# Splitting a weight chunk in two operations per helper engine rather than four

## The chip, the cores and the metric
The kernel runs on one core of one Trainium2 chip, as one launch. The metric is the device time of that launch in microseconds. A core has engines that work side by side, each in its own order and tied to the others by semaphores: TensorE (PE) for matmuls, with its weight loads shown apart as PEld; VectorE (DVE), ScalarE (ACT) and GpSimd (POOL) for elementwise work; SyncE (SP), which here issues nearly all loads.

## The reference
Two blocks run one after the other on 256 rows of 1024 features, all in float32. The first has two layers: modulated RMS norms, a mixer (differential attention beside neighbourhood attention in the first layer, grouped-query attention with sinks in the second), and a SwiGLU feed-forward; a context of 256 rows goes along in the first layer. The second block has four layers, and each of them is, cut to what matters:

```
for i in range(4):
    y = mixer_i(x)              # windowed attention, recurrent (RG-LRU), latent attention (MLA), windowed
    x = layer_norm(ALPHA * x + y, ...)
    x = layer_norm(ALPHA * x + cross_attention(x, mem_k, mem_v, x_w_q[i], x_w_o[i]), ...)
    h = causal_depthwise_conv(x @ f_w_up[i], ...)       # width 3, 2 x 2816 columns
    g, u = split(h)
    x = layer_norm(ALPHA * x + (silu(g) * u) @ f_w_down[i], ...)
```

Nearly all of the arithmetic is a product of 256 rows with a weight matrix that is used once. So every weight is read from HBM once, some 400 MB in all.

## The kernel before
**Products in two parts.** A float32 operand is written as hi + lo, where hi is its value in the engine's reduced float32 format (`F32R`) and lo what is left over. `mm3` (L137) then makes a product of three matmuls: hi by hi, hi by lo, lo by hi (L139, L140, L141). Activations are split by `split` (ACT makes hi at L157, DVE makes lo at L158), weights by `weights` (L125). A few first products of a stage skip the split and use plain float32 matmuls (`fp32_groups`, L110).

**Weights in chunks.** A weight matrix comes in chunks of 128 partitions by up to 2048 columns (1 MB). `raw` allocates a raw tile from a pool and SP loads it; `weights` allocates a hi and a lo tile and fills them piece by piece. For each piece ACT copies raw to hi (L133, tile `whi`), and DVE then subtracts hi from raw (L134, tile `wlo`). The piece width is set by one line:

```
h = (n // 4 + 63) // 64 * 64
```

With n = 2048 that gives four pieces of 512 columns on each engine; the 7 narrower chunks of the MLA block give four of 384 or 320. There are 296 chunks. A matmul waits only for the piece that holds its columns.

**Order.** The program is written stage by stage; a tile scheduler then lays out each engine's instructions in one fixed order. An engine takes them strictly in that order, so an instruction that waits holds up all behind it. `held` and `updates` (L85, L90) are lists of closures by which the program puts the tail of a norm behind later matmuls.

**The places that matter below.** The start of the program splits four chunks of memory weights, with nothing else for PE to do. `layer_norm` (L871) works on two halves of the rows: statistics on DVE (L890, L891), two small POOL operations (`rstd`, L175 and L176), the scaling of the row on DVE (L904, tile `r`), then transposes on PE (L165). `ffn` (L928) makes hidden tiles: `up` gives PSUM banks, `conv` scales them on ACT (L246, tile `cg`) and adds taps on DVE (L250); then SiLU (L954) and a product (L955) give `hf`, which is split into `hh` and `hl`; `down` takes these to the accumulators. The first two hidden tiles come from plain float32 matmuls (banks `s`); the chunks of the third and fourth (f = 2, 3) are split. `rglru` (L1071) has gates on ACT (L1108, L1114, L1115), products on POOL (L1117, L1118) and DVE operations (L1119 to L1121) for four groups, and the chunks of its last four projections are split in between.

Of the kernel before, what the change touches and what calls it, by code (L numbers as in the profile page):

```python
# [58 lines left out]
class Net:  # L59
# [65 lines left out]
    def weights(self, src, n=CW):  # L125
        nc = self.nc
        r = self.raw(src, n)
        hi = self.whl.tile([P, CW], F32R, tag="whi", name="whi")
        lo = self.whl.tile([P, CW], F32R, tag="wlo", name="wlo")
        h = (n // 4 + 63) // 64 * 64  # L130
        for a in range(0, n, h):
            b = min(a + h, n)
            nc.scalar.activation(hi[:, a:b], r[:, a:b], AF.Copy)  # L133
            nc.vector.tensor_tensor(lo[:, a:b], r[:, a:b], hi[:, a:b].bitcast(F32), op=ALU.subtract)  # L134
        return hi, lo
# [1513 lines left out]
```

## Time and profile before
| | |
|---|---|
| median of 3 runs | 2535.28 us (2532.03 to 2540.05) |
| the profiled execution | 2532.42 us; its span 2530.6 us |
| PE busy | 2468.5 us, 98% of the span |
| PEld busy | 2094.9 us, 83% |
| DVE busy | 1701.2 us, 67%, 3602 instructions |
| ACT busy | 1215.5 us, 48%, 2630 instructions |
| POOL busy | 130.8 us, 5% |
| lo pieces (L134) | 1184 instructions, 782.7 us, 688 ns each |
| hi pieces (L133) | 1184 instructions, 663.0 us, 620 ns each |
| mean load from HBM | 166 GB/s |

The page follows one execution. Busy shares are averages over stages; what ended an engine's idle time is named behind an arrow (`<-DVE wlo L134`: idle until that DVE instruction was done). A line of a helper such as L134 stands for all its callers.

### The profile page before, as it was taken

What the parts mean: (1) busy time and instruction counts of PE and PEld (TensorE: products, weight loads), DVE (VectorE), ACT (ScalarE), POOL (GpSimd) and SP (SyncE); (2) the same over time, 40 slices, a digit from 0 to 9 for tenths busy, and PEclk for the clock granted to TensorE, in tenths of its full rate; (3) what the DMA queues carried; (4) which work ended last, traced back from release to release, by engine and by line L of the source; (5) the groups of instructions that cost most, each with busy time, mean ns of one, the idle gap of its engine ahead of it and who ended that gap; (6) DMA issues with size and microseconds to landing.
All of it is one profiled execution on the core that took longest, in us unless ns stands there. A gap on an engine that the chain in (4) does not pass through costs nothing.

```text
span 2530.6 us, 39877 instructions
## 1 busy us (share of the span) xinstructions
PE 2468.5 (98%) x15706; PEld 2094.9 (83%) x15706; DVE 1701.2 (67%) x3602; ACT 1215.5 (48%) x2630; POOL 130.8 (5%) x172
## 2 busy tenths in 40 slices
PE   7999999999999999999999999999999999999998
PEld 5967658777788679986899988999878999769998
DVE  5463674343348765568787789677877777986777
ACT  4242353222235544446455665465555455564664
POOL 2000001111100000000000010000000000000000
PEclk9999999999999999999999999999999999999999
DMA  9415325343223545543545545355344455433653
GB/s 391 170 50 212 123 74 183 138 151 142 95 84 134 212 158 212 195 169 133 183 167 186 189 150 224 117 219 194 135 154 184 151 199 186 171 143 125 234 176 115
DMA packets 63708, 419.31 MB, mean 166 GB/s; under 512 B 7440, under 2 KB 7696, under 8 KB 16928
## 3 DMA queue, kind: packets, MB, share of 16 engines
q1 hardware_dynamic: 62240, 412.56, 44.9%
q0 software_dynamic: 1280, 4.20, 0.5%
q8 instruction: 123, 2.02, 0.3%
q14 instruction: 65, 0.53, 0.1%
HBM read 411.45 MB, written 5.28 MB: 165 GB/s over the span
## 4 chain that ended last, share of the span: by engine, by line
PE 87%; DVE 8%; ACT 3%; issue 1%; POOL 1%; DMA 0%; POOLq 0%; DVEq 0%; ACTq 0%
PE banka L139 9%; PE banka L140 9%; PE banka L141 9%; PE banks L139 6%; PE banks L141 6%; PE banks L140 6%; PE bankb L141 5%; PE bankb L140 5%; PE bankb L139 5%; PE bankt L165 3%; PE banko L139 2%; PE banko L141 2%; PE banks L110 2%; PE banko L140 2%; DVE wlo L134 2%; PE bankt L141 2%
## 5 line engine op out<-in xcount | busy, mean ns | idle before, releaser
L134 DVE TENSOR_TENSOR wlo<-raw,whi 128x512 fp32r<-128x512 f32 (+1 forms) x1184 | 782.7, 688 | 288.0 <-ACT whi L133 285.0
L133 ACT ACTIVATE whi<-raw 128x512 fp32r<-128x512 f32 (+1 forms) x1184 | 663.0, 620 | 638.7 <-issue 175.7
L141 PE MATMUL banks<-Th,wlo 128*128 128x256 f32 x880 | 249.5, 284 | 3.0 <-DVE wlo L134 3.0
L139 PE MATMUL banks<-Th,whi 128*128 128x256 f32 x880 | 249.3, 283 | 0.6 <-DVE uf L250 0.6
L140 PE MATMUL banks<-Tl,whi 128*128 128x256 f32 x880 | 249.1, 283 | 0.0
L141 PEld LDWEIGHTS banks<-Th,wlo 128*128 128x128 f32 x880 | 168.8, 192 | 4.1 <-DVE wlo L134 4.1
L139 PEld LDWEIGHTS banks<-Th,whi 128*128 128x128 f32 x880 | 168.8, 192 | 1.7 <-issue 0.7
L140 PEld LDWEIGHTS banks<-Tl,whi 128*128 128x128 f32 x880 | 168.8, 192 | 0.8
L139 PE MATMUL banka<-whi,Th 128*128 128x512 f32 (+1 forms) x304 | 122.2, 404 | 2.6 <-ACT Th L157 2.0
L140 PE MATMUL banka<-wlo,Th 128*128 128x512 f32 (+1 forms) x304 | 120.1, 398 | 2.0 <-DVE wlo L134 2.0
L655 DVE TENSOR_TENSOR sg<-sg,bankb 128x512 f32<-128x512 f32 x22 | 15.1, 688 | 158.4 <-PE bankb L141 158.4
L141 PE MATMUL banko<-Th,wlo 128*128 128x256 f32 x424 | 120.9, 285 | 0.6 <-DVE wlo L134 0.6
L139 PE MATMUL bankt<-Th,whi 128*128 128x256 f32 x424 | 120.3, 284 | 0.0
L141 PE MATMUL bankt<-Th,wlo 128*128 128x256 f32 x424 | 120.0, 283 | 0.0
L140 PE MATMUL bankt<-Tl,whi 128*128 128x256 f32 x424 | 120.0, 283 | 0.0
L139 PE MATMUL banko<-Th,whi 128*128 128x256 f32 x424 | 120.0, 283 | 0.0
L140 PE MATMUL banko<-Tl,whi 128*128 128x256 f32 x424 | 119.9, 283 | 0.0
L141 PE MATMUL banka<-whi,Tl 128*128 128x512 f32 (+1 forms) x304 | 117.9, 395 | 0.3 <-DVE Tl L158 0.3
L139 PE MATMUL bankb<-Th,whi 128*128 128x256 f32 (+1 forms) x344 | 115.0, 335 | 0.0
L141 PE MATMUL bankb<-Th,wlo 128*128 128x256 f32 (+1 forms) x344 | 114.7, 334 | 0.0
L140 PE MATMUL bankb<-Tl,whi 128*128 128x256 f32 (+1 forms) x344 | 114.2, 332 | 0.0
L157 ACT ACTIVATE hh<-hf 128x256 fp32r<-128x256 f32 x110 | 45.7, 415 | 136.2 <-DVE hf L955 135.2
(489 smaller groups left out, 6355.4 us busy)
## 6 DMA issues: line engine op xcount, KB each, us to landing
raw<-in_f_w_up_dram SPq DMA_DIRECT2D x88, 1024.0 KB, 4.8
raw<-in_ffn_w_dram SPq DMA_DIRECT2D x66, 1024.0 KB, 4.8
adaw<-in_ada_w_dram SPq DMA_DIRECT2D x48, 1024.0 KB, 4.8
raw<-in_f_w_down_dram SPq DMA_DIRECT2D x44, 1024.0 KB, 4.8
raw<-in_x_w_q_dram SPq DMA_DIRECT2D x16, 1024.0 KB, 4.8
raw<-in_x_w_o_dram SPq DMA_DIRECT2D x16, 1024.0 KB, 5.5
raw<-in_w_in_ab_dram SPq DMA_DIRECT2D x12, 1024.0 KB, 5.3
raw<-in_a_w_qkv_dram SPq DMA_DIRECT2D x12, 1024.0 KB, 4.9
```

The source lines that it names most:

```text
L110: self.nc.tensor.matmul(ps[:, f * S + t * P : f * S + (t + 1) * P], r[:, k * n * P + f * P : k * n * P + (f + 1) * P], xv[:, k, ts], start ...
L133: nc.scalar.activation(hi[:, a:b], r[:, a:b], AF.Copy)
L134: nc.vector.tensor_tensor(lo[:, a:b], r[:, a:b], hi[:, a:b].bitcast(F32), op=ALU.subtract)
L139: mm(out, l[0], r[0], start=start, stop=False)
L140: mm(out, l[0], r[1], start=False, stop=False)
L141: mm(out, l[1], r[0], start=False, stop=stop)
L157: nc.scalar.activation(hi, src, AF.Copy)
L165: self.nc.tensor.transpose(out, src, self.ident[:k, :k])
L655: nc.vector.tensor_tensor(sg, sg, ps[1], op=ALU.mult)
```

## The change
Four becomes two: a chunk's hi is made by two ACT operations of 1024 columns and its lo by two DVE operations of 1024 (for the narrower chunks two of 768 or 640). Nothing else is edited.

```
-        h = (n // 4 + 63) // 64 * 64
+        h = (n // 2 + 63) // 64 * 64
         for a in range(0, n, h):
             b = min(a + h, n)
             nc.scalar.activation(hi[:, a:b], r[:, a:b], AF.Copy)
             nc.vector.tensor_tensor(lo[:, a:b], r[:, a:b], hi[:, a:b].bitcast(F32), op=ALU.subtract)
```

DVE and ACT have 592 instructions fewer each; POOL's order is the same, PE's has the same matmuls, with several hundred of them in another place. The scheduler lays the engines' order out anew.

The first place is DVE in the second half of the norm after the first windowed attention (`st`, `mv` and `r` are the norm's tiles). Before:

```order
1073 L889 SCALAR_TENSOR_TENSOR r<-xs,bankb 128x512 x2
1074 L890 BN_STATS st<-r 128x6 x2
1075 L134 TENSOR_TENSOR wlo<-raw,whi 128x512
1076 L891 BN_AGGR mv<-st 128x2
1077 L134 TENSOR_TENSOR wlo<-raw,whi 128x512
1078 L904 TENSOR_SCALAR r<-r,mv,rs 128x512 x2
```

The changed kernel's DVE in the same place:

```order
1034 L889 SCALAR_TENSOR_TENSOR r<-xs,bankb 128x512 x2
1035 L890 BN_STATS st<-r 128x6 x2
1036 L134 TENSOR_TENSOR wlo<-raw,whi 128x1024
1037 L891 BN_AGGR mv<-st 128x2
1038 L158 TENSOR_TENSOR Tl<-xv,Th 128x4x128
1039 L904 TENSOR_SCALAR r<-r,mv,rs 128x512 x2
```

A piece of 1024 columns now stands ahead of L891, and the lo of an activation (Tl, 512 columns) in place of a weight piece behind it.

The second place is ACT at the start of the feed-forward of the second layer of the second block; the same pattern stands at the other three. Before:

```order
740 L157 ACTIVATE Th<-xv 128x4x128 x2
741 L246 ACTIVATE cg<-banks,fm 128x256 x2
742 L133 ACTIVATE whi<-raw 128x512
743 L954 ACT_TABLE_LOAD
744 L954 ACTIVATE hf<-cg 128x256
745 L246 ACTIVATE cg<-banks,fm 128x256 x2
746 L157 ACTIVATE hh<-hf 128x256
747 L133 ACTIVATE whi<-raw 128x512 x3
748 L954 ACTIVATE hf<-cg 128x256
749 L133 ACTIVATE whi<-raw 128x512 x4
```

The changed kernel's ACT there:

```order
716 L157 ACTIVATE Th<-xv 128x4x128 x2
717 L133 ACTIVATE whi<-raw 128x1024 x2
718 L246 ACTIVATE cg<-banks,fm 128x256 x2
719 L954 ACT_TABLE_LOAD
720 L954 ACTIVATE hf<-cg 128x256
721 L246 ACTIVATE cg<-banks,fm 128x256 x2
722 L157 ACTIVATE hh<-hf 128x256
723 L133 ACTIVATE whi<-raw 128x1024 x2
724 L954 ACTIVATE hf<-cg 128x256
725 L133 ACTIVATE whi<-raw 128x1024
```

The whole chunk of f = 3 (one piece of it before) now stands ahead of the scaling of the first hidden tile, L246.

The third place is DVE in the recurrent block, at its second and third group. Before:

```order
1437 L1119 TENSOR_SCALAR sq<-r 128x512
1438 L1120 SCALAR_TENSOR_TENSOR a_13812<-a_13812,r 128x512
1439 L134 TENSOR_TENSOR wlo<-raw,whi 128x512
1440 L1121 SCALAR_TENSOR_TENSOR a_13812<-a_13812,r 128x512
1441 L134 TENSOR_TENSOR wlo<-raw,whi 128x512 x2
1442 L1119 TENSOR_SCALAR sq<-r 128x512
1443 L1120 SCALAR_TENSOR_TENSOR a_13915<-a_13915,r 128x512
```

The changed kernel's DVE there:

```order
1351 L1119 TENSOR_SCALAR sq<-r 128x512
1352 L1120 SCALAR_TENSOR_TENSOR a_13166<-a_13166,r 128x512
1353 L134 TENSOR_TENSOR wlo<-raw,whi 128x1024
1354 L1121 SCALAR_TENSOR_TENSOR a_13166<-a_13166,r 128x512
1355 L1119 TENSOR_SCALAR sq<-r 128x512
1356 L1120 SCALAR_TENSOR_TENSOR a_13307<-a_13307,r 128x512
```

Pieces two, three and four of that chunk, which stood around L1121, have become one operation ahead of it, the chunk's second half; the first half stands before this place.

## Rows read from the trace of the kernel before
**Rows 1.** The page's busy times (engine, us, share, instructions) and its chain by engine
```profile
PE 2468.5 (98%) x15706; PEld 2094.9 (83%) x15706; DVE 1701.2 (67%) x3602; ACT 1215.5 (48%) x2630; POOL 130.8 (5%) x172
PE 87%; DVE 8%; ACT 3%; issue 1%; POOL 1%; DMA 0%; POOLq 0%; DVEq 0%; ACTq 0%
```
**Rows 2.** A stretch: its length, busy PE, PEld, DVE, ACT, POOL, then clock, DMA
```profile
2087.70:2151.00 63.30, 63.30 (x466) 60.43 (x465) 44.68 (x88) 36.61 (x75) 0.00 (x0) 1.00 0.53 186
```
**Rows 3.** What PE waited for: us in total, times, longest us
```profile
PE banka L139 <- ACT whi L133: 12.9, 3, 8.8
PE bankt L165 <- DVE r L904: 8.1, 7, 2.2
PE banka L140 <- DVE wlo L134: 4.3, 6, 1.2
PE banks L141 <- DVE wlo L134: 3.4, 6, 1.1
```
**Rows 4.** Groups by shape: busy us, mean ns, idle before and its releasers
```profile
L134 DVE TENSOR_TENSOR wlo<-raw,whi 128x512 fp32r<-128x512 f32 x1156 | 769.1, 692 | 288.0 <-ACT whi L133 285.0
L133 ACT ACTIVATE whi<-raw 128x512 fp32r<-128x512 f32 x1156 | 650.9, 623 | 629.1 <-issue 175.7 <-PE bankb L140 118.0 <-PE banka L140 72.8
```
**Rows 5.** Timeline of the start, DVE and ACT: start us, duration us, operation
```profile
7.52 2.29 DVE L158 TENSOR_TENSOR meml<-raw,memh 128x2048 fp32r<-128x2048 f32 x1 [6.37 <-ACT memh L157]
9.73 2.49 DVE L134 TENSOR_TENSOR wlo<-raw,whi 128x512 fp32r<-128x512 f32 x4
...
5.58 1.91 ACT L157 ACTIVATE memh<-raw 128x2048 fp32r<-128x2048 f32 x1 [3.57 <-DMA raw<-in_memT_dram]
```
**Rows 6.** Timeline of the start, PE's first lo matmuls of two memory chunks
```profile
10.46 0.58 PE L141 MATMUL banka<-memh,wlo 128*128 128x256 f32 x1
...
40.56 0.39 PE L141 MATMUL banka<-memh,wlo 128*128 128x256 f32 x1 [0.22 <-DVE wlo L134]
```
**Rows 7.** Timeline of the first norm of the second block: POOL, DVE, PE
```profile
1206.38 0.19 POOL L175 TENSOR_SCALAR rs<-mv 128x1 f32<-128x1 f32 x1 [75.03 <-DVE mv L891]
...
1216.92 0.52 POOL L175 TENSOR_SCALAR rs<-mv 128x1 f32<-128x1 f32 x1 [9.72 <-DVE mv L891]
...
1216.75 0.63 DVE L134 TENSOR_TENSOR wlo<-raw,whi 128x512 fp32r<-128x512 f32 x1
...
1218.71 0.66 PE L165 MATMUL bankt<-cst,r 128*128 128x128 f32 x4 [1.13 <-DVE r L904]
```
**Rows 8.** Timeline of the second convolution block's start: ACT, DVE, PE
```profile
1641.33 1.02 ACT L246 ACTIVATE cg<-banks,fm 128x256 f32<-128x256 f32 x2 [1.82 <-PE banks L110]
1646.57 0.63 ACT L133 ACTIVATE whi<-raw 128x512 fp32r<-128x512 f32 x1 [4.23 <-DMA raw<-in_f_w_up_dram]
...
1654.52 0.41 DVE L158 TENSOR_TENSOR hl<-hf,hh 128x256 fp32r<-128x256 f32 x1
...
1652.13 0.38 PE L141 MATMUL banko<-Th,wlo 128*128 128x256 f32 x1 [0.55 <-DVE wlo L134]
...
1657.51 0.40 PE L139 MATMUL banka<-whi,hh 128*128 128x512 f32 x1
```
**Rows 9.** Timeline of the recurrent block: DVE, PE
```profile
1512.06 0.68 DVE L134 TENSOR_TENSOR wlo<-raw,whi 128x512 fp32r<-128x512 f32 x1
...
1512.79 0.39 PE L141 MATMUL banks<-Th,wlo 128*128 128x256 f32 x1 [1.13 <-DVE wlo L134]
...
1515.69 0.39 PE L141 MATMUL banks<-Th,wlo 128*128 128x256 f32 x1 [0.71 <-DVE wlo L134]
```
**Rows 10.** Timeline of PE around eight transposes, in a full stretch
```profile
1464.99 0.40 PE L141 MATMUL bankb<-whi,hl 128*128 128x512 f32 x1
1465.22 0.60 PE L165 MATMUL bankt<-cst,r 128*128 128x128 f32 x4
1465.66 0.60 PE L165 MATMUL banko<-cst,r 128*128 128x128 f32 x4
1466.02 0.48 PE L139 MATMUL bankb<-whi,hh 128*128 128x512 f32 x1
```

More of the change, by code (lines that the diff above doesn't have):

```diff
@@ L129, in weights @@
         lo = self.whl.tile([P, CW], F32R, tag="wlo", name="wlo")
-        h = (n // 4 + 63) // 64 * 64
+        h = (n // 2 + 63) // 64 * 64
         for a in range(0, n, h):
```

## The prediction
> **What bounds the kernel now.** I read the page's busy shares and its chain first. TensorE (PE) is busy for 2468.5 of 2530.6 us and carries 87% of the chain that ended last; VectorE (DVE) carries 8%, ScalarE (ACT) 3% [rows 1]. Next came busy time by stretch: in the middle of a feed-forward block PE is busy for 63.30 of 63.30 us while DVE has 44.68 and ACT 36.61 of work [rows 2]. So over most of the span the splitting of weights is hidden, and a saving there buys nothing. Then I read what PE waits for. Its lines that name split pieces are hi for 12.9 us in 3 waits (8.8 of it the start of the program, before anything has been split), lo for 4.3 in 6 and 3.4 in 6; a norm's scaling (`r`, L904) holds it for 8.1 us in 7 waits [rows 3]. Those places decide the sign; the 1184 + 1184 pieces in between do not.
>
> **What a wider piece costs.** A 512-column lo takes 692 ns and hi 623 ns [rows 4]; a 2048-column operation of the same kind takes 2.29 us on DVE and 1.91 on ACT [rows 5]. So 512 more columns cost (2.29 - 0.69)/3 = 0.53 us on DVE and (1.91 - 0.62)/3 = 0.43 on ACT, and a 1024-column piece takes about 1.22 and 1.05 us. Four queued lo pieces take 2.49 us together [rows 5], a step of 0.60 us each; two of 1024 columns take 0.60 + 0.53 + 1.22 = 2.35. That is 0.14 us a chunk, some 40 us of DVE over 296 chunks and, by the same working, somewhat more on ACT. I cost it at nothing where PE is full; PE hides it there. What is on the path is the first piece of a chunk: its hi comes 0.43 later, and its lo 0.53 later if hi was early, 0.96 if not.
>
> **The start, +1.5 us.** PE takes its first lo at 10.46, right behind the first lo piece, which starts at 9.73 because DVE is busy until then; it will end 0.53 later [rows 5, 6]. The fourth memory chunk finds PE waiting again, lo arriving at 40.56 [rows 6]; there nothing covers hi, so +0.96. PE runs without a gap behind both, and nothing takes it back. Bounds 0.5 (hi hidden in both) and 2.8 (a third such wait soon after, which I take to be covered by other work that ends as late).
>
> **The norms, +3.1 us.** In a norm's second half DVE does statistics, a lo piece, the aggregate (L891), another lo piece, and then L904, which needs two small POOL operations. PE ran out of work at 1218.71 and had waited 1.13 us for L904 [rows 7]. The order puts a 1024-column piece in the place of the first 512 one, and a Tl of 512 columns in the place of the second. So L891 and all behind it is 0.53 later. Of the seven such waits four have this form or its mirror image (the wide piece behind L891): 4 x 0.53 = 2.1. Two more, at the MLA block and at the last attention block, get wide pieces in both places, but PE's order has 5 to 8 more matmuls ahead of the transposes there; I take +0.5 each. For the seventh, in the recurrent block, the order has a wide piece and 4 more matmuls to cover it; I take nothing. Bounds: -1 (the covered cases repaid) and +5.
> The row also shows that POOL is not independent of DVE: its first operation takes 0.19 us with DVE idle and 0.52 beside a lo piece, ending just behind it [rows 7]. If that is a fixed loss, a wide piece costs no more there; if POOL waits for the end of the piece, a wide one behind L891 costs another 0.53. I take the second, and it is in the 3.1; by the first the term would be 2.1.
> The Trainium skill (SBUF — State Buffer, Who interferes with whom) says that a DVE instruction with two SBUF inputs holds a read interface that GpSimd needs, for its whole length. A lo subtract reads raw and hi from SBUF, and the row agrees: 0.52 against 0.19. By this rule longer pieces block POOL longer; it speaks against the change.
>
> **The four convolution blocks, -1.2 us.** At 1646.57 ACT splits one piece of the chunk that has just landed, and then turns to the table load and the hidden columns; the other three pieces come later, and PE waits at 1652.13 for lo [rows 8]. In the changed order ACT splits the whole chunk first, so this wait goes: -0.6 here, and I take -0.6 for the other three starts together, where the order is the same. The price: the scaling of the first hidden tile (L246), which ran at 1641.33, now stands behind that DMA and two wide pieces, until 1646.57 + 1.9 = 1648.5, or 7.2 us later. The second hidden tile had its lo part (hl) at 1654.9; PE starts on hidden tiles at 1657.51 [rows 8] and on the second of them 6 matmuls of 0.23 [rows 10] later, at 1658.9. Followed through the new order of ACT and DVE, with the old durations and wide pieces of 1.05 and 1.22, hl comes at about 1658, where PE, 0.6 to 1.0 earlier, asks for it. I take that as just in time. Bounds -1.6 and the rival below.
>
> **The recurrent block, -1.5 us.** PE waits there for pieces two, three and four of a chunk, 1.13 and 0.71 us at the first and the last [rows 9]. Before, one piece of that chunk was done early; now a whole half is, and the other half is one operation in the place where piece two stood (1512.06). It ends near 1513.3, so the last quarter can start near 1514.1 instead of 1515.69 [rows 9]. The next chunk takes part of it back, as DVE pieces beside POOL's products are slowed. Bounds -2.5 and +1.
>
> **PE's own order, +1.0 us.** The scheduler re-sorts; PE changes from one kind of matmul to another some 20 times more often. Into the transposes a switch costs 0.44 - 0.36 = 0.08 us [rows 10], and about as much out of them: 20 x 0.08 = 1.6 if all are in full stretches, 0 if none. I take 1.0.
>
> **Other lo waits, +1.0 us.** Four of the waits in [rows 3] are at first pieces elsewhere; between nothing (the wide piece stands earlier in the order) and +0.96 each, I take a quarter.
>
> **Sum.** 1.5 + 3.1 - 1.2 - 1.5 + 1.0 + 1.0 = +3.9 us. The profiled execution took 2532.4 us (its span 2530.6 and 1.8 around it), 2.9 below the median of the runs; so 2536.3 for a like execution and 2539 for the median, +0.15%.
>
> **Rivals.**
> *Slower, the convolution blocks.* ACT works in order, so the whole chain of the first hidden tiles waits for a weight chunk's DMA. If all 7.2 us reach the second tile, of which 1658.9 - 1654.9 = 4.0 is slack, PE loses 3.2 at each of four starts and wins nothing there: about +13 in the place of -1.2, or 2553. It decides once hl of the second tile is over about 1 us later than I followed it. Against it: ACT has idle time in front of the DMA, and part of the 7.2 is the table load's old wait for the same DMA.
> *Slower, latency everywhere.* All lo waits grow by 0.96 and every norm by 0.53 to 1.06, with the norms that PE does not wait for today joining in: 12 x 0.96 + 2 x 0.43 + 12 x 0.53 = +19 at most, with the gains left in about +14: 2549. For it: PE has no slack to give back. Against it: in the cross-attention norms the piece behind L891 goes away, and 0.33 of the 0.53 with it.
> *Faster, relief of DVE.* The chain has 8% on DVE, some 200 us, though most of that is not splitting. If the helpers' saved 40 and more us shorten their queues wherever PE waits, the lo lines (7.7) and half of the norm line go: -12, or 2524. For it: in the recurrent block DVE is near full. Against it: where PE waits, DVE has mostly just received its input, and the latency of one piece counts, not the sum.
> *Nothing happens*: all terms are small and cancel, 2535; this lies within the forecast's own case.
>
> **How the numbers follow.** About 0.3%, 7.6 us, is what a measurement here can tell from no change. My forecast, with all sums from -7 to +7 around no change, has 0.60; its own range, from the terms' bounds taken not all at one end, is 2531 to 2545. The convolution rival has 0.11, latency 0.15, relief 0.14. So faster 0.14, same 0.60, slower 0.26. The range 2529 to 2550 leaves out the far ends of both sides.
>
> **What would show it right or wrong.** In the new profile L134 and L133 have 592 instructions each, of 1.22 and 1.05 us, and their busy time falls by some 40 to 100 us on each engine with PE's busy time unchanged. The first lo matmul is at about 11.0, L904 waits are longer at 1218, 1475, 1927 and 2271 by half a microsecond each, and PE's first wait for lo in the convolution blocks is gone. If PE waits there for hl or hh, the first rival is on. If the lo lines and the L904 line among PE's waits both shrink, I was wrong, and relief is right.

## The result and the profile after

The changed kernel takes 2551.53 us (median of 4 runs, 2549.99 to 2554.46), the kernel before 2533.84 in the same comparison: ratio 1.0069, interval 1.0058 to 1.0081. It is slower by 17.7 us, outside the predicted range and on the side to which I had given 0.26.

The helpers did what was worked out. The page's busy line and chain, then the two groups of pieces by shape (busy us, mean ns, idle before):

```profile
PE 2474.5 (97%) x15706; PEld 2100.0 (82%) x15706; DVE 1670.0 (66%) x3010; ACT 1164.3 (46%) x2038; POOL 133.3 (5%) x172
PE 85%; DVE 10%; ACT 2%; issue 2%; POOL 1%; DMA 1%; POOLq 0%; DVEq 0%; ACTq 0%
...
L134 DVE TENSOR_TENSOR wlo<-raw,whi 128x1024 fp32r<-128x1024 f32 x578 | 705.2, 1231 | 368.7 <-ACT whi L133 366.7
...
L133 ACT ACTIVATE whi<-raw 128x1024 fp32r<-128x1024 f32 x578 | 596.9, 1053 | 751.0 <-PE bankb L141 138.9 <-issue 129.8 <-PE banks L140 128.1
```

A piece takes 1.23 and 1.05 us; DVE has 31 us less to do, ACT 51. PE is busy for 6.0 us more (2474.5 against 2468.5) and idle for 12.1 more; together they are the 18.1 us by which the profiled span grew (2548.7 against 2530.6). Against [rows 1] the chain moved from PE (87 to 85%) to DVE (8 to 10%). What PE waits for, beside [rows 3]:

```profile
PE bankt L165 <- DVE r L904: 15.1, 12, 2.8
PE banka L139 <- ACT whi L133: 14.2, 3, 9.3
PE banks L141 <- DVE wlo L134: 4.1, 4, 1.5
PE banka L140 <- DVE wlo L134: 4.0, 5, 1.4
```

These two lo lines hardly moved; with the smaller ones, PE's waits for a lo went from 8.5 to 10.6 us. The norm's line nearly doubled, 8.1 us in 7 waits to 15.1 in 12. The first norm of the second block, beside [rows 7]: first two rows of before (PE's last matmul into the accumulator, and the norm's first DVE operation), then DVE, POOL and PE of the changed kernel.

```profile
1213.62 0.39 PE L141 MATMUL bankb<-whi,Tl 128*128 128x512 f32 x1
1213.65 1.27 DVE L889 SCALAR_TENSOR_TENSOR r<-xs,bankb 128x512 f32<-128x512 f32 x2
```
```profile
1220.53 1.21 DVE L134 TENSOR_TENSOR wlo<-raw,whi 128x1024 fp32r<-128x1024 f32 x1
1221.67 1.27 DVE L889 SCALAR_TENSOR_TENSOR r<-xs,bankb 128x512 f32<-128x512 f32 x2
...
1224.06 1.20 DVE L134 TENSOR_TENSOR wlo<-raw,whi 128x1024 fp32r<-128x1024 f32 x1
1225.19 0.20 DVE L891 BATCH_NORM_AGGREGATE mv<-st 128x2 f32<-128x12 f32 x1
1225.31 0.63 DVE L158 TENSOR_TENSOR Tl<-xv,Th 128x512 fp32r<-128x512 f32 x1
1226.66 1.00 DVE L904 TENSOR_SCALAR r<-r,mv,rs 128x512 f32<-128x512 f32 x2 [0.72 <-POOL rs L176]
...
1225.47 0.52 POOL L175 TENSOR_SCALAR rs<-mv 128x1 f32<-128x1 f32 x1 [13.51 <-DVE mv L891]
...
1221.26 0.39 PE L141 MATMUL bankb<-whi,Tl 128*128 128x512 f32 x1
...
1227.26 0.66 PE L165 MATMUL bankt<-cst,r 128*128 128x128 f32 x4 [2.04 <-DVE r L904]
```

The wait of 1.13 became 2.04. Of these 0.91 us, 0.53 are the wider piece ahead of L891: from the start of L889 to that of L904 it is 4.99 us, where it was 4.46 (1213.65 to 1218.11). The other 0.38 stand ahead of L889: it starts 0.41 us behind the start of PE's last matmul into the accumulator, where it had been 0.03, because DVE was in the middle of another wide piece. And then something happened that had not before: the busy time by stretch around it (length, PE, PEld, DVE, ACT, POOL, then the granted clock), of the changed kernel and then of the kernel before, reads

```profile
1221.65:1227.26 5.61, 3.58 (x34) 3.38 (x32) 4.89 (x10) 2.04 (x3) 1.07 (x2) 1.00 0.43 147
1227.26:1229.00 1.74, 1.65 (x11) 1.37 (x12) 1.74 (x3) 1.13 (x5) 0.00 (x0) 0.89 0.96 405
1229.00:1232.00 3.00, 3.00 (x16) 3.00 (x16) 2.92 (x7) 1.71 (x4) 0.00 (x0) 0.50 0.14 60
1232.00:1236.00 4.00, 4.00 (x36) 4.00 (x36) 2.58 (x5) 0.60 (x1) 0.00 (x0) 1.00 0.71 248
```
```profile
1218.71:1222.00 3.29, 3.20 (x23) 2.77 (x24) 3.29 (x8) 2.99 (x8) 0.00 (x0) 1.00 0.40 72
```

Behind the wait PE worked at the lower of its two levels, 1.2 GHz, for over 3 us: 16 matmuls in 3 us where the next 4 us hold 36. By an estimate from these rows the fall cost 0.5 x 3.00 + 0.11 x 1.74 = 1.7 us more, nearly twice what the wait itself had grown. Behind the same norm before, the clock had stayed at 2.4 GHz. The mean granted clock of the execution went from 0.996 to 0.991. Over the span that is some 13 us of full-speed time, which is more than the falls cost, since it also counts time in which PE waits.

The worst of the norms, between the first convolution block and the recurrent block: PE's last matmul into the accumulator, DVE, POOL, and the wait; then the wait of before, and the stretch behind the longer one.

```profile
1479.82 0.39 PE L141 MATMUL bankb<-whi,hl 128*128 128x512 f32 x1
...
1486.58 0.66 PE L165 MATMUL bankt<-cst,r 128*128 128x128 f32 x4 [2.80 <-DVE r L904]
...
1479.85 1.22 DVE L134 TENSOR_TENSOR wlo<-raw,whi 128x1024 fp32r<-128x1024 f32 x1
1480.98 1.28 DVE L889 SCALAR_TENSOR_TENSOR r<-xs,bankb 128x512 f32<-128x512 f32 x2
...
1484.08 1.17 DVE L134 TENSOR_TENSOR wlo<-raw,whi 128x1024 fp32r<-128x1024 f32 x1
...
1484.26 1.05 POOL L175 TENSOR_SCALAR rs<-mv 128x1 f32<-128x1 f32 x1 [10.11 <-DVE mv L891]
```
```profile
1475.41 0.66 PE L165 MATMUL bankt<-cst,r 128*128 128x128 f32 x4 [1.49 <-DVE r L904]
```
```profile
1488.00:1491.00 3.00, 3.00 (x15) 2.96 (x15) 2.92 (x7) 2.02 (x5) 0.00 (x0) 0.50 0.48 202
```

The wait was 1.49 before. A wide piece begins at 1479.85, just as the accumulator is finished, and L889 starts only at 1480.98, 0.77 us after the accumulator's last matmul ends (1480.21); before, it had started at once. A second wide piece holds POOL's L175 for 1.05 us where a 512-column one had held it for 0.52. Together 0.77 + 0.53 = 1.30, and 2.80 - 1.49 = 1.31.

The norm's line grew by 7.0 us in all. Of these 4.3 are at four norms: the two above (0.91 and 1.31) and the ones behind the MLA block and the last windowed attention (0.94 and 1.10). PE waited 2.0 to 2.8 us at each of them, and behind each the clock fell. Another 1.7 are at the four norms behind cross-attention, ahead of the convolution blocks, where PE had not waited before and now waits 0.43 or 0.44 each. The one of the second layer:

```profile
1646.60 0.66 PE L165 MATMUL bankt<-cst,r 128*128 128x128 f32 x4 [0.44 <-DVE r L904]
```

The start, beside [rows 6], a stretch of it, and a row of before:

```profile
10.97 0.58 PE L141 MATMUL banka<-memh,wlo 128*128 128x256 f32 x1 [0.55 <-DVE wlo L134]
...
41.89 0.39 PE L139 MATMUL banka<-memh,whi 128*128 128x256 f32 x1 [1.63 <-ACT whi L133]
...
43.15 0.38 PE L141 MATMUL banka<-memh,wlo 128*128 128x256 f32 x1 [0.76 <-DVE wlo L134]
...
44.00:46.00 2.00, 2.00 (x12) 0.36 (x10) 0.85 (x7) 1.48 (x2) 0.00 (x0) 0.54 1.02 430
```
```profile
39.84 0.38 PE L139 MATMUL banka<-memh,whi 128*128 128x256 f32 x1 [1.20 <-ACT whi L133]
```

The first lo matmul came 0.51 us later, as worked out; the one of the fourth chunk 2.6 later. PE's waits for that chunk grew by 0.43 for hi and 0.54 for lo, as worked out too, but behind them the clock fell. The convolution block and the recurrent block, beside [rows 8, 9]:

```profile
1664.86 0.42 DVE L158 TENSOR_TENSOR hl<-hf,hh 128x256 fp32r<-128x256 f32 x1
...
1667.99 0.40 PE L139 MATMUL banka<-whi,hh 128*128 128x512 f32 x1
...
1526.30 0.39 PE L141 MATMUL banks<-Th,wlo 128*128 128x256 f32 x1 [1.48 <-DVE wlo L134]
```

In the convolution block hl of the second hidden tile ends 2.7 us before PE begins with hidden tiles: the rival that feared ACT's order is out. PE's wait for lo there (0.55 us) is gone. In the recurrent block the five waits for lo (3.0 us) are three (2.9 us).

### The profile page after: what moved, and what is told of

The parts are those of the page before. It is cut to its first block, busy times and chain, and to the rows that moved or that the text cites. A ratio compares the mean times of both kernels' runs of the same rounds, so it can differ in the third digit from the quotient of the medians.

```text
span 2548.7 us, 38745 instructions
## 1 busy us (share of the span) xinstructions
PE 2474.5 (97%) x15706; PEld 2100.0 (82%) x15706; DVE 1670.0 (66%) x3010; ACT 1164.3 (46%) x2038; POOL 133.3 (5%) x172
## 4 chain that ended last, share of the span: by engine, by line
PE 85%; DVE 10%; ACT 2%; issue 2%; POOL 1%; DMA 1%; POOLq 0%; DVEq 0%; ACTq 0%
PE banka L139 9%; PE banka L141 9%; PE banka L140 9%; PE banks L139 6%; PE banks L141 6%; PE banks L140 6%; PE bankb L141 4%; PE bankb L140 4%; PE bankb L139 4%; PE bankt L165 3%; DVE wlo L134 3%; PE banko L139 2%; PE banks L110 2%; PE banko L140 2%; PE banko L141 2%; PE bankt L140 2%
## 5 line engine op out<-in xcount | busy, mean ns | idle before, releaser
L134 DVE TENSOR_TENSOR wlo<-raw,whi 128x1024 fp32r<-128x1024 f32 (+1 forms) x592 | 717.6, 1223 | 368.7 <-ACT whi L133 366.7
L133 ACT ACTIVATE whi<-raw 128x1024 fp32r<-128x1024 f32 (+1 forms) x592 | 607.6, 1048 | 761.6 <-PE bankb L141 144.1
L655 DVE TENSOR_TENSOR sg<-sg,bankb 128x512 f32<-128x512 f32 x22 | 15.1, 688 | 156.8 <-PE bankb L141 156.8
L139 PE MATMUL banka<-whi,hh 128*128 128x512 f32 x240 | 94.2, 393 | 0.0
```

The source lines that it names most:

```text
L139: mm(out, l[0], r[0], start=start, stop=False)
L655: nc.vector.tensor_tensor(sg, sg, ps[1], op=ALU.mult)
```

## The experiments

All ratios are against the kernel before on the same chip, 5 rounds each; the last column is the ratio applied to 2533 us.

| run | pieces (hi, lo) | ratio, interval | us against before |
|---|---|---|---|
| e1 | 2, 4 | 1.0027, 1.0015 to 1.0039 | +7 |
| e2 | 4, 2 | 1.0077, 1.0063 to 1.0091 | +20 |
| e4 | 2, 2, lo behind L904 | 1.0077, 1.0065 to 1.0089 | +20 |
| e5 | 4, 4, lo behind L904 | 1.0065, 1.0053 to 1.0077 | +16 |
| e6 | 4 near norms, else 2 | 1.0036, 1.0022 to 1.0050 | +9 |
| e7 | 2 near norms, else 4 | 1.0035, 1.0023 to 1.0047 | +9 |
| e3 | 2 in five feed-forwards, else 4 | 1.0003, 0.9994 to 1.0011 | +1 |
| e8 | 2, 2, 12 matmuls in four waits | 1.0068, 1.0056 to 1.0080 | +17 |
| f1 | 2, 2, 6 matmuls in four waits | 1.0051, 1.0038 to 1.0064 | +13 |
| f2 | 2 in the first block, else 4 | 1.0028, 1.0018 to 1.0037 | +7 |
| f3 | 8 near norms, else 4 | 0.9980, 0.9970 to 0.9991 | -5 |
| f4 | 8, 8 | 1.0001, 0.9992 to 1.0010 | 0 |

**Which engine's pieces** (e1, e2). `weights` with different widths on the two engines:

```
+        hh, hl = ((n // p + 63) // 64 * 64 for p in (2, 4))     # e2: (4, 2)
...
+            for c in range(a, e, hh): ...                        # hi pieces of this part, ACT
+            for c in range(a, e, hl): ...                        # lo pieces of this part, DVE
```

> hi in two operations of 1024 columns on ACT, lo still in four of 512 on DVE. In the order every second half of a norm again has 512-column lo pieces around L891. Theory A (the wide lo piece lengthens DVE's part of the norms, PE waits longer there and then runs some microseconds at the lower clock): nearly all of the 17.7 us is gone; 0 to +5 against before, L904 line of PE's waits at 8 to 10 us, no clock dips behind the norms of the second block that before did not have. Theory B (the later hi pieces on ACT and the pieces they hold up): +10 to +18. Theory C (fewer instructions, and so another order of the scheduler, whatever the engine): about half, +6 to +11.

> lo in two operations of 1024 columns on DVE, hi still in four of 512 on ACT. In the order the norms have the wide pieces as in the changed kernel. Theory A (norms and clock): most of the loss stays, +11 to +18; L904 line 13 to 16 us, dips of the clock behind four or more norms. Theory B (hi on ACT): 0 to +6. Theory C: +6 to +11.

Wide lo alone brings all of the loss, a little more than A allowed, and B is out. Wide hi alone brings +7, more than A allowed and within what C had. The two don't add up (27 against 17.7). One thing they share: in both the clock falls at the start behind the fourth memory chunk, as it does in each of the eight profiled executions with wide hi or lo there and in none of the other six. In e1's trace the norm's line is back at 8.5 us, and what is left lies ahead of the second block: its first L175 comes 10.3 us later than before (at 1216.68), its end 9.0.

**Lo pieces queued behind the norm** (e4, e5). Ahead of the other split, I tried to clear the norm's chain:

```
+            with self.tc.issue_after(gate.ins) if gate else ExitStack():   # gate: the norm's last L904
                 nc.vector.tensor_tensor(lo[:, a:b], r[:, a:b], hi[:, a:b].bitcast(F32), op=ALU.subtract)
```

> The changed kernel (two pieces on both engines), and DVE's lo pieces of the three chunks that are traced behind a norm are queued behind that norm's last L904, so no weight piece stands between L890 and L904; nothing else differs. Theory A: the L904 line falls below that of before (8.1 us), to 2 to 6, the dips of the clock behind the norms go, and the time is -4 to +6 against before; the +3.5 us of the start stays. Theory B or C: the time stays at +12 to +18, or grows as lo comes later.

> The kernel before (four pieces on both engines) with the same queueing of lo pieces behind L904. Theory A: the L904 line falls from 8.1 to 2 to 5 us and the time by 2 to 8 us. Theory B or C: no change within 3 us, or slower as lo comes later for the first matmuls behind the norm.

Both miss, and the profile of e5 says why. At the first norm, DVE and PE (L904 is L908 here, L201 is L205), and then PE at the norm ahead of the MLA block:

```profile
1218.46 4.90 DVE L138 TENSOR_TENSOR wlo<-raw,whi 128x512 fp32r<-128x512 f32 x8
...
1218.14 0.66 PE L169 MATMUL bankt<-cst,r 128*128 128x128 f32 x4 [0.61 <-DVE r L908]
...
1223.74 4.48 PE L111 MATMUL banka<-xv,raw 128*128 128x128 f32 x24 [2.17 <-DVE xv L205]
...
1832.60 1.11 PE L169 MATMUL bankt<-cst,r 128*128 128x128 f32 x4 [2.81 <-DVE r L908]
```

The first norm itself got faster (PE waits 0.61 in the place of 1.13), but eight lo pieces that had been held back then went ahead of L205, for 4.90 us in a row, and PE waited 2.17 us for that. At the norms ahead of the MLA block and the last attention PE waited 2.81 and 3.63 us, where it had waited 0.56 and 0.29. So the norm's line rose, to 10.2 us in e5 and 12.5 in e4, where A had at most 6. By the letter both came out as B or C had it, slower as lo comes later. But the edit shortened some waits and made longer ones in other places; as a test of A it decides nothing.

**Where the width counts** (e6, e7, e3, f2). The width by place in place of the order:

```
-        h = (n // 4 + 63) // 64 * 64
+        h = (n // (4 if self.near else 2) + 63) // 64 * 64       # e7: 2 if near else 4; f3: 8 if near else 4
+        self.near = max(self.near - 1, 0)                        # set to 3 behind each L904
```

e3 gives `weights` a width of its own in `ffn`'s calls; f2 has two pieces in every call up to the second block, four behind.

> The changed kernel, but the first three chunks that are traced behind each row half of a layer norm (some 36 of 296) go in four pieces as before; the other chunks in two. In the order every norm of the second block again has one 512-column piece on each side of the aggregate, as before the change. Theory A (a wide lo piece in the norm's chain on DVE makes PE wait longer, and after the longer waits PE runs at the lower clock): L904 line 8 to 10 us, no dips behind the norms but that of the recurrent block, and +3 to +8 us against before (start and first block remain). Theory C (fewer instructions and another order all over): +13 to +18. Theory B (wide hi pieces as such): +10 or more.

> The reverse: the kernel before, with two pieces only for those three chunks behind each row half of a layer norm. Theory A: most of the loss comes with these 36 chunks, +8 to +14 us, L904 line 13 to 17 us, dips of the clock behind three or more norms. Theory C: a ninth to an eighth of the loss, +1 to +3.

> Two pieces only for the chunks of the five feed-forwards behind the second layer's mixer (155 of 296), four for all others. These chunks stand where PE is full, and in the norms behind cross-attention, where PE hardly waits. Theory A: -2 to +4 us against before. Theory C: in proportion to the pieces merged, +7 to +11.

> Two pieces in the first block (start, both mixers, SwiGLU, its second feed-forward), four in the whole second block. Theory A, with the same mechanism at the start and in the first block's norms: what the run with four pieces near the norms left over, +6 to +10 us, nearly all of it before 1230 us of the span, and none of it behind. Theory C: in proportion to the pieces, +5 to +8, but spread. Against both: under +3, the left-over came from the second block after all.

Their lines for the norm, of e6, e7 and f2 in this order:

```profile
PE bankt L167 <- DVE r L906: 8.5, 8, 1.9
```
```profile
PE bankt L167 <- DVE r L906: 15.3, 10, 3.4
```
```profile
PE bankt L166 <- DVE r L905: 8.0, 7, 2.2
```

The chunks behind norms (33, by 66 DVE instructions fewer in e7) bring +9 alone (e7) and all of the norm's line; left narrow, they take about 9 of the 17.7 away (e6). 155 chunks in feed-forwards bring nothing that can be told from zero (e3), although the norm's line rose there too, by the waits behind cross-attention:

```profile
PE bankt L165 <- DVE r L904: 10.7, 11, 2.5
```

The first block brings +7 with a norm's line as before (f2); in its profile the second block's first L175 comes 10.7 us later than before (at 1217.08) and the end 10.1, where in e7's it is 0.2 (at 1206.54) and 10.7. 9 + 7 is near 17.7, so the two places account for nearly all of the loss. C, a loss in proportion to the pieces merged, is out by e3 and e7. A was too low on the first block's share in e6 (+9 where I had +3 to +8); e3, e7 and f2 came as A had them.

**The clock** (e8, f1). Matmuls whose result is overwritten, ahead of the transposes of the four norms where PE waited 2.0 to 2.8 us:

```
+        for _ in range(warm):                                    # 12 in e8, 6 in f1
+            self.nc.tensor.matmul(ps[:, :P], self.ident, self.ident, start=True, stop=True)
         for i in range(4):
             self.transpose(ps[:, i * P : (i + 1) * P], src[:, i * P : (i + 1) * P])
```

> The changed kernel with twelve matmuls more (identity by identity, into the bank that the transposes overwrite next) ahead of the transposes in the second half of four norms, where PE waited 2.0 to 2.8 us for L904 and its granted clock fell behind the wait. They take about 1.4 us of a wait that is longer, so the transposes start no later and no earlier. If the fall of the clock is a cause of its own (part of theory A): the four dips of 1.7 us go, -5 to -8 against the changed kernel, +9 to +13 against before. If only the waits count: no difference, +16 to +20 against before.

> The run with twelve extra matmuls again, with six at each of the four norms (six take 1.4 us by the run before, where twelve took 2.84 and so outlasted the waits of 2.0 to 2.8 us). Transposes start when they did in the changed kernel. If the fall of the clock is a cause of its own: the four dips go, L904 line about 9 to 10 us, -4 to -8 us against the changed kernel, so +10 to +14 against before. If only the waits count: +16 to +20 against before.

At the first norm of e8 the twelve took 2.84 us and outlasted the wait:

```profile
1228.03 2.84 PE L192 MATMUL bankt<-cst 128*128 128x128 f32 x24
1230.71 0.60 PE L165 MATMUL bankt<-cst,r 128*128 128x128 f32 x4
```

From PE's last matmul into the accumulator to these transposes it is 6.48 us, where it was 6.00 in the changed kernel; at the four norms together that is 1.1 us. The clock stayed up behind all four, where the four falls had cost some 6.8 by the estimate above. Yet e8 takes as long as the changed kernel (+17), which is what was expected if only the waits count. In its profile the clock fell in other places, at 347, 1528, 1870 and 2204 us among them.

f1 has six there, which fit; L165 again starts when L904 is done, and in the profile the clock stays up at all four:

```profile
1229.81 1.50 PE L192 MATMUL bankt<-cst 128*128 128x128 f32 x12
1231.97 0.66 PE L165 MATMUL bankt<-cst,r 128*128 128x128 f32 x4 [0.66 <-DVE r L906]
```

By the ratio it is 12.9 us slower than before where the changed kernel is 17.7, within what was expected if the fall is a cause of its own. But the intervals of the two overlap (1.0038 to 1.0064 and 1.0058 to 1.0081), the medians differ by 3 us, and e8 shows no gain. The traces show that the falls are gone from the four places and how slowly PE worked in them; that their time comes back in the whole is not shown.

**The other way** (f3, f4).

> The kernel before, with the three chunks behind each row half of a layer norm in eight pieces of 256. By theory A each second half of a norm gains 0.27 us ahead of L891, 0.2 to 0.3 where POOL waits for a piece, and up to 0.27 where a piece is in progress as the accumulator ends: PE's L904 line falls from 8.1 to 4 to 5 us and the time by 2 to 6 us. Theory C (more instructions, another order): 0 to +3.

> Eight pieces of 256 columns for every chunk. By theory A, latency counts and helper time is hidden: -3 to -8 us against before, the first lo matmul of the program some 0.3 us earlier, L904 line 4 to 5 us, though DVE is busy for some 80 us more. By the opposite reading (helper time counts) +10 or more.

f3 beats both kernels: 0.9980 against before, a small gain whose interval is clear of 1. Its first norm on DVE, POOL and PE, and the line of its waits:

```profile
1215.43 0.41 DVE L136 TENSOR_TENSOR wlo<-raw,whi 128x256 fp32r<-128x256 f32 x1
...
1216.05 0.25 POOL L177 TENSOR_SCALAR rs<-mv 128x1 f32<-128x1 f32 x1 [9.53 <-DVE mv L893]
...
1217.57 0.66 PE L167 MATMUL bankt<-cst,r 128*128 128x128 f32 x4 [0.68 <-DVE r L906]
...
PE bankt L167 <- DVE r L906: 5.8, 7, 1.9
```

Every term shrinks with the piece: 0.41 us ahead of the aggregate, 0.25 on POOL, a wait of 0.68. f4, narrow everywhere, gains nearly the same at the norms (6.3 us for 8.1) and gives it back. One place is the recurrent block, with a single wait for lo of 3.7 us:

```profile
PE banks L141 <- DVE wlo L134: 4.8, 2, 3.7
```

In f4's profile another 4.5 us are lost ahead of the second block (its first L175 at 1210.84); what costs them stays open. So narrow pieces everywhere win nothing, where I had expected -3 to -8; why they cost time is shown in part only.

## Why the prediction was wrong

**What bounds the kernel**: right. e3 merges the pieces of 155 chunks, nearly all in full stretches, for +1 us with an interval around zero. That PE's busy time would not change was wrong: it rose by 6.0 us.

**The cost of a piece**: right, 1.23 and 1.05 us against 1.22 and 1.05. DVE's busy time fell by 31 us, a little less than the 40 worked out.

**The norms, +3.1**: the step that failed. The mechanism was named and its place was right, but the term was mis-sized threefold: the chunks behind norms cost some 9 us (e7, and e6 the other way round). (In [rows 7], 1218.71 is where PE's wait ends; its work had ended 1.13 us earlier.) Its two parts that I had came as worked out. The piece ahead of L891 cost 0.53 at the first norm. POOL is held to the end of the piece: its L175 took 0.19 us alone, and in the changed kernel 0.52 beside 512 columns and 1.05 beside 1024. By the fixed loss that I weighed against it, the second would have been 0.52 too. The Trainium skill (SBUF — State Buffer, SBUF: two separate sides) has the whole DVE instruction as the time for which GpSimd is shut out, and this case agrees at 0.25 us for 256 columns also.

Three parts were missing. First, DVE finished a piece that it had begun, in both norms shown: where the accumulator ends behind the start of a wide piece, L889 waits for the rest of it, 0.38 us at the first norm and 0.77 at the worst. With it the four waits that I had at 0.53 each grew by 0.91, 1.31, 0.94 and 1.10. Second, the four norms behind cross-attention, where I had PE not waiting, now make it wait 0.43 or 0.44 each. So the norm's line rose by 7.0 us, not 3.1. Third, PE's clock fell behind the four longer waits, an estimated 1.7 us a time in the two places shown (3 us at 0.50 each), and behind these norms it had not fallen before. I had read the granted clock only as a mean of 0.996, and taken matmul times as fixed. How much of the 9 us is the clock is not settled by e8 and f1.

**The start, +1.5, and the other waits, +1.0**: too low. Start and first block together cost some 7 us (f2), not 2 to 3. At the start the two waits that I counted grew as worked out (0.51, and 0.97 for 0.96); what had no term is the clock's fall behind the second of them, and the third wait, which I took to be covered, grew by 0.5 (hi 2.85 to 3.28, lo 1.25 to 1.36). How the rest divides over the first block's norms and attention, and what part of it the wide hi pieces have by themselves (e1), stays open.

**The convolution blocks, -1.2, and the recurrent block, -1.5**: neither gain is there. In the first the wait for lo went as worked out, but it was the only one of the four starts (0.55 us), and the norms ahead of the four blocks took back 1.7; e3, which has these blocks, is at +1. In the second the waits are fewer, but those left are longer (1.48 us where the longest was 1.13), so the sum hardly changed.

**PE's own order, +1.0**: not told apart by any run.

**The rivals**: the convolution rival is out. The latency rival (2549) comes nearest in time, and its reason, that PE has no slack to give back, holds, and so does its part that norms without a wait join in; its even spread over all lo waits does not, since they grew by 2.1 us in all. Relief is out: the norm's line grew.

## What to carry to other kernels

Size the pieces of background work by the place where they run: where the main engine is full, the width is free; where it waits for a chain on the helper, the rest of the piece in progress, the piece in the order and an operation that is held until the piece ends each add to the wait. When the main engine waits a few tenths longer, look at its granted clock behind the wait before taking the wait for the whole cost.

## What the runs showed that was not expected

The clock's fall is not a fixed answer to a wait. Up to 355 us the changed kernel and f1 have the same instructions in the same order, and the same wait of 1.8 us at 345 us; the ten microseconds behind it, of the changed kernel and then of f1:

```profile
345.00:355.00 10.00, 9.96 (x56) 6.82 (x56) 8.84 (x19) 4.48 (x10) 0.00 (x0) 1.00 0.10 26
```
```profile
345.00:355.00 10.00, 9.25 (x34) 6.07 (x35) 7.07 (x16) 4.72 (x11) 0.00 (x0) 0.55 0.07 26
```

One stayed at 2.4 GHz, the other lost some 4.5 us (0.45 x 10, an estimate). The clock fell here in 12 of the 14 profiled executions, that of the kernel before among them; in e7's it did not fall behind waits of 2.40 and 2.20 us at norms. So one profile shows which waits can bring a fall, and not how often they do. It also means that in f1's profiled span the falls that are gone from the four places are in part made up by what it lost here.
